# Weight tiles that start at 64 or 192 bytes from the moving operand, output projections by 256 columns, and the dilated q, k, v units by two matmuls of 256

## The chip, the cores and the metric

The kernel runs on one core of one Trainium2 chip. The metric is the device time of one execution in microseconds (us); the time of the kernel before is the median of three.

## What is computed

The input is 256 tokens of width 1024 in float32. Two blocks of two layers each follow one another. Shortened from the reference:

```python
def first_block(x, ...):                       # two layers
    h = rms_norm(x, norm_mix[l]);  proj = h @ w_in[l]
    y_a = dilated_attention(dq, dk, dv) @ w_proj_a[l]      # 3 dilations x 4 heads of 64
    y_b = stick_breaking_attention(sq, sk, sv) @ w_proj_b[l]
    x = x + (gates_a * y_a + gates_b * y_b) @ w_out[l]
    x = x + conv_ffn(rms_norm(x, norm_ffn[l]), w_up, conv_w, conv_b, w_down)   # 1024 -> 2*2816 -> 1024
def second_block(x, mem, ...):                 # layer 0 even_mixer, layer 1 odd_mixer
    x = x + rms_norm_2(mixer(rms_norm_2(x, g[0])), g[1])
    x = x + rms_norm_2(memory_cross_attention(h, mem, ...), g[3])
    x = x + rms_norm_2(square(relu(h @ mlp_w1[l])) @ mlp_w2[l], g[5])          # 1024 -> 4096 -> 1024
```

## The kernel before

**Layout.** An activation lies transposed: 128 features on the partitions, 256 tokens along the free axis, eight chunks of features for width 1024. A projection multiplies weight chunks (128 x 128, the stationary operand, loaded into TensorE by a LDWEIGHTS) with such chunks (128 x 256, the moving operand that streams past).

**Three matmuls for one product.** Each float32 operand is held as a high part in the type fp32r and a low part, the rest. `mm3` (L240) makes a product of three matmuls: high weight by high activation, low weight by high activation, high weight by low activation. So a chunk of 256 tokens is three matmuls of 256 columns, each with a weight load of its own. Nearly all of TensorE's work comes from `mm` (L236), which `mm3` calls.

**The weight stream.** `plan` writes out every block of weights in the order of use, mostly 512 KB each. `prep` (L188) loads block i into a tile raw by DMA and splits it in two halves: ScalarE copies a half to its high part (L199), VectorE subtracts to get the low part (L200). A half is one tile w of the pool tag "w", which has eight buffers (`WB = 8`). `take` hands a block out and prepares up to five blocks ahead.

**Where the tiles stand.** A buffer of tag "w" is as large as the largest tile that asks for it: 4160 bytes on each partition. The program places the eight at bytes 39552, 43712, 47872, 52032, 56192, 60352, 64512 and 68672, which is 128, 192, 0 and 64 modulo 256, twice over. The activations' high and low parts are tiles xh: four buffers of tag "xs" (the input of w_in, w_up, the mixers and w1), all at 128 modulo 256, and sixteen of tag "hs" (the input of all output projections), all at 64. High and low parts, chunks and column blocks within these tiles lie multiples of 256 bytes apart (but for two units of 260 columns). Below, the *distance* of a pair is the start of the moving operand less that of the stationary operand, modulo 256. Before the change it takes the values 0, 64, 128 and 192 about equally often.

**The output projections** (w_out, w_down, w2, and the last four chunks of the mixers' outputs) run in `proj_tail` (L367): for each of eight output chunks c, k steps over the input chunks. For c below 7, `mm3_wide` (L245) takes two matmuls a step: the high weight by the high and low activation side by side (512 columns), then the low weight by the high activation (256 columns). The result stands in two halves of a PSUM bank, which the part's reader adds: in the first block two VectorE additions (L875, L877), in the second a ScalarE copy and a VectorE addition (L1343, L1344). Chunk 7 goes by `mm3`.

**The dilated q, k, v units** (`proj_n` with C = 512, called by `unit`, L697) have it the other way round: the activation's chunk of 128 tokens is stationary and 512 columns of the weight stream past, three matmuls of 512 columns a step.

**Order.** The tile framework schedules all engines' instructions by a simulated timeline, so the order in the source is not the order in the queues. Where attention runs, transposes, scores and sums in plain float32 stand between the matmuls of the projections; in w_up, w_down, w1 and w2 the projections' matmuls follow each other by hundreds.

Of the kernel before, what the change touches and what calls it, by code (L numbers as in the profile page):

```python
# [33 lines left out]
LEAD = 5  # L34
WB = 8
TCARGS = dict(schedule_with_timeline_sim=True)
SET_EXP = "natural_log_exp_and_others"
# [78 lines left out]
def starts(blocks):  # L116

    out = [0]
    for _, _, nk, _, C in blocks:
# [3 lines left out]

BUFS = {"x": 5, "xs": 4, "hs": 16, "ft": 7, "sq": 2, "p": 6, "bias": 3, "row": 4, "sm": 16, "mk": 2, "mv": 2,
        "mm": 2, "sc": 2, "pT": 2, "pv": 1, "ms": 1}
# [3 lines left out]
def net(ctx, tc, A, out):  # L129
# [5 lines left out]
    pp = ctx.enter_context(tc.tile_pool(name="psum", bufs=1, space=PSUM))  # L135
    dp = ctx.enter_context(tc.tile_pool(name="dram", bufs=1, space=DRAM))

    def f(x):
# [49 lines left out]
    def prep(i, pieces=1):  # L188
# [7 lines left out]
        for a, b in ((0, h), (h, nk)):  # L196
            if a < b:
                w = wp.tile([P, 2, b - a, C], F32R, tag="w", name=f"w{i}", bufs=WB)
                act.activation(w[:, 0], raw[:, a:b], AF.Copy)  # L199
                dve.tensor_tensor(w[:, 1], raw[:, a:b], f(w[:, 0]), op=OP.subtract)  # L200
                ready[i] += [w[:, :, k] for k in range(b - a)]
# [38 lines left out]
    def mm3(o, l, r, start, stop=True):  # L240

        for n, (a, b) in enumerate(((0, 0), (1, 0), (0, 1))):
            mm(o, l[:, a], r[:, b], start and n == 0, stop and n == 2)

    def mm3_wide(o, l, r, start, stop):  # L245

        mm(o, l[:, 0], r, start, False)
        mm(o[:, 0:T], l[:, 1], r[:, 0], False, stop)

# [73 lines left out]

    def proj_wide(name, c0, x, k, tag):

        ps = bank(tag, "mw")
        for k0 in range(0, k, 8):
            w = take(name, c0, k0)
            for kk in range(min(8, k - k0)):
                mm3_wide(ps.rearrange("p a t -> p (a t)"), w[kk], x(k0 + kk), start=(k0 + kk == 0),  # L330
                         stop=(k0 + kk == k - 1))
        return ps

    def proj_n(name, c0, x, C=256, tag="mm"):

        if C <= 256:
            ps = bank(tag, "mm")
            outs = [ps[:, 0], ps[:, 1]]
        else:
            outs = [bank(tag, "mm", (C,)), bank(tag, "mm", (C,))]  # L340
        step = 2 if C > 260 else 4
        for k0 in range(0, KC, step):
            w = take(name, c0, k0)
            for kk, i in order(step):
                k = k0 + kk
                mm3(outs[i], cut(x(k), col(i)), w[kk], start=(k == 0 and (i == 0 or C > 256)), stop=(k == KC - 1))
        return outs
# [18 lines left out]

    def proj_tail(name, x, k, on_part, tags=("mm", "sc", "mm", "sc", "mm", "sc", "mm", "sc"), first=0):  # L367

        for c in range(first, 8):
            if c == 4:  # L370
                hold(True)
            if c < 7:
                ps = proj_wide(name, 128 * c, x, k, tags[c])
                on_part(c, ps[:, 0], ps[:, 1])
            else:
                on_part(c, proj_c(name, 128 * c, x, k, tags[c]), None)

# [235 lines left out]


    h = Split("xs")
    for c in range(8):
        split_last = h.chunk(c, x[c // 2][:, c % 2], vcol(V_MIX + c))

    def first_sums():
# [5 lines left out]
        return ns  # L625

    exchange = const("exchange", [P, P], nc.gpsimd)
    table = const("table", [32, 28], nc.gpsimd)
# [39 lines left out]
    for l in range(DEPTH):  # L668
        vb = l * V_L1
        w_in = f"w_in{l}"  # L670
        def rope_unit(nat):
            ra = sb("sm", "ra", (2, 4, 2, 8))
            rb = sb("sm", "rb", (2, 4, 2, 8))
            for i in range(2):
# [190 lines left out]
        def residual(w, y, k, gains):  # L865
# [4 lines left out]

            def on_part(c, a, b):
                if c % 2 == 0:
                    xn.append(sb("x", f"x{c // 2}"))
                t = xn[c // 2][:, c % 2]
                state["block1"] = dve.tensor_tensor(t, x[c // 2][:, c % 2], a, op=OP.add).ins  # L875
                if b is not None:
                    dve.tensor_tensor(t, t, b, op=OP.add)  # L877
                if c < 6 and c % 2:
                    ns.pair(xn[c // 2])
                if hn is not None:  # L880
                    hn.chunk(c, t, gains(c))
                if c >= 6:
                    ns.chunk(t)

# [75 lines left out]

    lprod = sb("sm", "lp", (64,))
    lsum = sb("sm", "ls", (2,))
# [347 lines left out]
    class Output:  # L1310
# [24 lines left out]

        def part(self, c, a, b):
            if b is None:
                self.chunk(c, a)
                return
            if c % 2 == 0:  # L1340
                self.ys.append(sb("ft", "y"))
            y = self.ys[c // 2]
            act.activation(y[:, c % 2], b, AF.Copy)  # L1343
            dve.tensor_tensor(y[:, c % 2], a, y[:, c % 2], op=OP.add)  # L1344
            if c == 6:
                self.sums.chunk(y[:, 0])
                self.scale(y[:, 0], y[:, 0], c)
            elif c % 2:
                self.sums.pair(y)
                for i in range(2):  # L1350
                    self.scale(y[:, i], y[:, i], c - 1 + i)

# [16 lines left out]
    for l in range(DEPTH):  # L1369
        name, oo, of = even(h, nrm) if l == 0 else odd(h, nrm)  # L1370
        y = Output(lambda c: gain2(l, 1, c), 2)
        for j in range(2):
            y.pair(j, of.banks[j])
        proj_tail(name, oo, KC, y.part, tags=(None,) * 4 + ("sc", "mm", "sc", "mm"), first=4)
        r = y.sums.rows(1)
# [158 lines left out]
```

## Time and profile before

| | us |
|---|---|
| median of 3 runs | 1434.24 (1433.52 to 1435.65) |
| the profiled execution, its own time | 1434.43 |
| its span, first to last instruction | 1432.3 |
| TensorE busy in the span | 1388.8 (97%) |
| VectorE busy | 1019.8 (71%) |
| ScalarE busy | 886.3 (62%) |

The span lies 2.1 us inside the execution's own time, and that time is 0.2 us from the median. A matmul's row in the profile gives how long one takes from its start to its end; matmuls overlap, so what one adds to the time is the spacing of the starts, which a stretch's length over its count gives.

### The profile page before, as it was taken

How to read it: one execution, taken by the hardware profiler on the slowest of the kernel's cores; microseconds unless marked ns; L12 is line 12 of the kernel's file. 1: busy time of each engine (PE TensorE's matmuls, PEld its weight loads, DVE VectorE, ACT ScalarE, POOL GpSimd, SP SyncE). 2: the span in 40 equal slices, each digit the busy share in tenths (PEclk: the TensorE clock that was granted, in tenths of full speed). 3: DMA queues.
4: the chain of work that ended last, by engine and by line, in shares of the span. 5: the costliest groups of instructions: out<-in, count | busy, mean ns of one | idle time of the engine just before them, and what ended most of it. 6: DMA issues, size and time to landing. Idle time of an engine off the chain costs nothing.

```text
span 1432.3 us, 26226 instructions
## 1 busy us (share of the span) xinstructions
PE 1388.8 (97%) x9950; PEld 1270.7 (89%) x9950; DVE 1019.8 (71%) x2140; ACT 886.3 (62%) x1740; POOL 27.3 (2%) x54
## 2 busy tenths in 40 slices
PE   8999999999999999999999989899999999899997
PEld 6789999998888999999899968799989878799886
DVE  6665888886656578888777786777656876777554
ACT  6666566665566666666656656566556676576553
POOL 1000000000000000000000010000000010000000
PEclk9999999999999999999999989999999999999999
DMA  7543566556653455656655553266656534265662
GB/s 247 187 124 119 182 195 191 188 177 188 192 170 119 127 172 188 193 190 198 198 167 164 154 139 118 75 190 186 186 187 180 161 94 133 82 186 189 182 189 85
DMA packets 69326, 236.14 MB, mean 165 GB/s; under 512 B 7954, under 2 KB 12322, under 8 KB 69200
## 3 DMA queue, kind: packets, MB, share of 16 engines
q1 hardware_dynamic: 67136, 229.24, 51.6%
q0 software_dynamic: 1920, 5.04, 1.8%
q8 instruction: 78, 1.28, 0.4%
q14 instruction: 48, 0.39, 0.1%
q10 hardware_dynamic: 144, 0.19, 0.0%
HBM read 233.35 MB, written 1.09 MB: 164 GB/s over the span
## 4 chain that ended last, share of the span: by engine, by line
issue 53%; PE 39%; DVE 3%; ACT 3%; DMA 1%; POOL 0%; SPq 0%; DVEq 0%; POOLq 0%; ACTq 0%
PE mm L236 21%; PE mw L236 12%; PE mo L236 2%; PE ssum L427 1%; PE pT L483 1%; PE sc L607 1%; PE sc L604 1%; ACT w L199 1%; DVE w L200 1%; PE pv L541 1%; DMA bias<-brel_d 1%; DMA x<-in_xT_dram 0%; ACT rstd L176 0%; ACT sq L431 0%; ACT px L176 0%
## 5 line engine op out<-in xcount | busy, mean ns | idle before, releaser
L200 DVE TENSOR_TENSOR w<-raw,w 128x512 fp32r<-128x512 f32 (+2 forms) x866 | 585.3, 686 | 303.3 <-ACT w L199 292.8
L199 ACT ACTIVATE w<-raw 128x512 fp32r<-128x512 f32 (+2 forms) x866 | 535.5, 626 | 414.6 <-PE mm L236 225.5
L236 PE MATMUL mm<-xh,w 128*128 128x256 f32 x5892 | 722.8, 283 | 7.8 <-ACT xh L1000 6.8
L236 PEld LDWEIGHTS mm<-xh,w 128*128 128x128 f32 x5892 | 703.7, 190 | 21.2 <-ACT xh L1000 8.4
L236 PE MATMUL mw<-xh,w 128*128 128x512 f32 (+1 forms) x1832 | 327.3, 339 | 2.4 <-DVE xh L271 1.4
L236 PEld LDWEIGHTS mw<-xh,w 128*128 128x128 f32 x1832 | 281.2, 188 | 44.6 <-DVE xh L271 2.0
L236 PE MATMUL mm<-w,xh 128*128 128x512 f32 (+2 forms) x672 | 145.8, 372 | 9.5 <-ACT w L199 7.0
L236 PEld LDWEIGHTS mm<-w,xh 128*128 128x128 f32 x672 | 113.6, 191 | 34.0 <-ACT w L199 8.4
L236 PE MATMUL mo<-xh,w 128*128 128x256 f32 x192 | 30.6, 307 | 0.5 <-ACT xh L513 0.5
L236 PEld LDWEIGHTS mo<-xh,w 128*128 128x128 f32 x192 | 26.5, 206 | 4.4 <-ACT xh L513 1.7
L1000 ACT ACTIVATE xh<-x,vec 128x256 fp32r<-128x256 f32 x48 | 22.6, 501 | 10.4 <-DVE x L1365 9.9
L497 POOL DMA_DIRECT2D bias<-brel_d x28 | 14.9, 538 | 680.0 <-DVE sbb L821 293.0
L905 ACT ACTIVATE ftt<-fa,vec 128x256 f32<-128x256 f32 x44 | 24.1, 594 | 2.3 <-DVE fa L900 0.5
L1003 DVE SCALAR_TENSOR_TENSOR xh<-x,vec,xh 128x256 fp32r<-128x256 f32 x48 | 22.1, 483 | 1.1 <-ACT xh L1000 1.1
L431 ACT ACTIVATE sq<-x 128x512 f32<-128x512 f32 x33 | 20.4, 617 | 2.3 <-DMA x<-in_xT_dram 2.1
L906 DVE SCALAR_TENSOR_TENSOR ftt<-fa,vec,ftt 128x255 f32<-128x255 f32 x44 | 20.9, 482 | 0.2
L907 DVE SCALAR_TENSOR_TENSOR ftt<-fa,vec,ftt 128x254 f32<-128x254 f32 x44 | 21.0, 477 | 0.0
L703 DVE TENSOR_TENSOR gate<-mm,rstd 128x512 f32<-128x512 f32 x16 | 11.1, 691 | 12.5 <-PE mm L236 12.5
L438 DVE TENSOR_TENSOR sq<-sq 128x512 f32<-128x512 f32 x26 | 17.9, 688 | 0.0
L176 ACT ACTIVATE ftt<-ftt 128x512 f32<-128x512 f32 x22 | 13.9, 631 | 6.4 <-DVE ftt L907 6.4
L1364 DVE TENSOR_TENSOR y<-y,rstd 128x512 f32<-128x512 f32 (+1 forms) x25 | 14.5, 581 | 4.3 <-ACT rstd L176 4.1
L910 DVE TENSOR_TENSOR fa<-mm,rstd 128x512 f32<-128x512 f32 x22 | 15.1, 687 | 3.1 <-PE mm L236 3.1
(413 smaller groups left out, 1137.2 us busy)
## 6 DMA issues: line engine op xcount, KB each, us to landing
raw<-in_wt_dram SPq DMA_DIRECT2D x411, 512.0 KB, 3.6
raw<-in_wt_dram SPq DMA_DIRECT2D x16, 384.0 KB, 3.5
bias<-brel_d POOLq DMA_DIRECT2D x28, 128.0 KB, 3.4
raw<-in_wt_dram SPq DMA_DIRECT2D x4, 520.0 KB, 3.5
mem<-in_memT_dram SPq DMA_DIRECT2D x8, 256.0 KB, 4.2
x<-in_xT_dram SPq DMA_DIRECT2D x4, 256.0 KB, 6.7
raw<-in_wt_dram SPq DMA_DIRECT2D x4, 256.0 KB, 3.3
out_dram<-y SPq DMA_DIRECT2D x4, 256.0 KB, 2.5
```

The costliest lines, as they stand in the source:

```text
L199: act.activation(w[:, 0], raw[:, a:b], AF.Copy)
L200: dve.tensor_tensor(w[:, 1], raw[:, a:b], f(w[:, 0]), op=OP.subtract)
L236: i = pe.matmul(o, a, b, start=start, stop=stop, skip_group_check=True).ins
L431: act.activation(sq, src, AF.Square)
L438: dve.tensor_tensor(self.acc, self.acc, sq, op=OP.add)
L497: nc.gpsimd.dma_start(o, src)
L905: act.activation(t[:, c], a[:, c], AF.Identity, bias=vcol(vb + V_CB + ch), scale=w[2])
L906: dve.scalar_tensor_tensor(t[:, c, 1:], a[:, c, :T - 1], w[1], t[:, c, 1:], op0=OP.mult, op1=OP.add)
L907: dve.scalar_tensor_tensor(t[:, c, 2:], a[:, c, :T - 2], w[0], t[:, c, 2:], op0=OP.mult, op1=OP.add)
L910: dve.tensor_tensor(a, o, over(rr), op=OP.mult)
L1000: act.activation(hi, t, AF.Copy, scale=g)
L1003: return dve.scalar_tensor_tensor(lo, t, g, f(hi), op0=OP.mult, op1=OP.subtract)
```

## The change

Four edits. The buffers of tag "w" become 1056 floats, 4224 bytes, and every weight tile is a view of one (`W_SLOT`). Two padding tiles, 192 and 64 bytes, go ahead of the activations' pools, and small scratch tiles get a tag of their own ("ro"). `proj_tail` uses `mm3` for all chunks and lets two chunks share a bank, so that chunks 0 to 5 are read out in pairs and 6 and 7 each alone. `proj_n` splits 512 columns into two times 256.

```diff
-BUFS = {..., "sm": 16, "mk": 2, ...
+W_SLOT = 1056
+BUFS = {..., "sm": 16, "ro": 4, "mk": 2, ...
...
+    def pad(name, n):
+        ap.tile([P, n // 4], F32, tag=name, name=name, bufs=1)
...
-                w = wp.tile([P, 2, b - a, C], F32R, tag="w", name=f"w{i}", bufs=WB)
+                w = wp.tile([P, W_SLOT], F32R, tag="w", name=f"w{i}", bufs=WB)
+                w = w[:, :2 * (b - a) * C].rearrange("p (s k c) -> p s k c", s=2, k=b - a)
...
                 k = k0 + kk
-                mm3(outs[i], cut(x(k), col(i)), w[kk], start=(k == 0 and (i == 0 or C > 256)), stop=(k == KC - 1))
+                for a in range(0, C, 256 if C > 260 else C):
+                    s = slice(a, a + (256 if C > 260 else C))
+                    mm3(outs[i][:, s], cut(x(k), col(i)), cut(w[kk], s),
+                        start=(k == 0 and a == 0 and (i == 0 or C > 256)), stop=(k == KC - 1))
...
-    def proj_tail(name, x, k, on_part, tags=("mm", "sc", "mm", "sc", "mm", "sc", "mm", "sc"), first=0):
+    def proj_tail(name, x, k, on_part, tags=("mm", "sc", "mm", "sc", "mm"), first=0):
+        tags = list(tags)
+        cs, ps = [], None
         for c in range(first, 8):
             if c == 4:
                 hold(True)
-            if c < 7:
-                ps = proj_wide(name, 128 * c, x, k, tags[c])
-                on_part(c, ps[:, 0], ps[:, 1])
-            else:
-                on_part(c, proj_c(name, 128 * c, x, k, tags[c]), None)
+            if not cs:
+                ps = bank(tags.pop(0), "mw", (2, T) if c < 6 else (1, T))
+            for k0 in range(0, k, 8):
+                w = take(name, 128 * c, k0)
+                for kk in range(min(8, k - k0)):
+                    mm3(ps[:, len(cs)], w[kk], x(k0 + kk), start=(k0 + kk == 0 and not cs),
+                        stop=(k0 + kk == k - 1))
+            cs.append(c)
+            if c % 2 or c >= 6:
+                on_part(cs, ps)
+                cs = []
...
+    pad("pad0", 192)
     h = Split("xs")
...
+    pad("pad1", 64)
...
-                state["block1"] = dve.tensor_tensor(t, x[c // 2][:, c % 2], a, op=OP.add).ins
-                if b is not None:
-                    dve.tensor_tensor(t, t, b, op=OP.add)
+                s = slice(c % 2, c % 2 + len(cs))
+                state["block1"] = dve.tensor_tensor(xn[c // 2][:, s], x[c // 2][:, s], ps, op=OP.add).ins
...
-            act.activation(y[:, c % 2], b, AF.Copy)
-            dve.tensor_tensor(y[:, c % 2], a, y[:, c % 2], op=OP.add)
```

After the change the program places the eight weight buffers at 39552, 43776, 48000 and so on to 69120, which is 128 and 0 modulo 256 in turn, and all twenty xh buffers at 64. So the distance is 64 or 192, whichever of the two operands streams (again but for the 260-column units).

TensorE's queue in the second weight block of an output chunk of w_down, layer 0, before the change (output bank, then stationary and moving tile; the first number after w is the block):

```order
L236 MATMUL mw_4066<-xh_2892,w109_3966 128x512
L236 MATMUL mw_4066<-xh_2892,w109_3966 128x256
L236 MATMUL mw_4066<-xh_2892,w109_3966 128x512
L236 MATMUL mw_4066<-xh_2892,w109_3966 128x256
L236 MATMUL mw_4066<-xh_3037,w109_3966 128x512
L236 MATMUL mw_4066<-xh_3037,w109_3966 128x256
```

The same place after the change, where w109_4307 and w109_4310 stand at 128 and w110_4333 at 0 modulo 256:

```order
L242 MATMUL mw_4431<-xh_3177,w109_4307 128x256 x6
L242 MATMUL mw_4431<-xh_3322,w109_4307 128x256 x6
L242 MATMUL mw_4431<-xh_3467,w109_4310 128x256 x6
L242 MATMUL mw_4431<-xh_3612,w109_4310 128x256 x6
L242 MATMUL mw_4431<-xh_3757,w110_4333 128x256 x6
```

A step over one input chunk was a matmul of 512 and one of 256 columns with two weight loads; it is three of 256 with three.

Six halves of weight blocks in w_up, layer 0, before the change, in TensorE's queue. The program places w65_2463 at 64 modulo 256, w65_2466 and w66_2495 at 192, w66_2498 at 128, w67_2538 at 0 and w67_2541 at 64, the moving xh at 128:

```order
L236 MATMUL mm_2605<-xh_2037,w65_2463 128x256 x12
L236 MATMUL mm_2605<-xh_2086,w65_2466 128x256 x12
L236 MATMUL mm_2680<-xh_1920,w66_2495 128x256 x12
L236 MATMUL mm_2680<-xh_1982,w66_2498 128x256 x12
L236 MATMUL mm_2680<-xh_2037,w67_2538 128x256 x12
L236 MATMUL mm_2680<-xh_2086,w67_2541 128x256 x12
```

The same after the change; w65_2748, w65_2751, w67_2823 and w67_2826 stand at 128, w66_2780 and w66_2783 at 0 modulo 256, the moving xh at 64:

```order
L242 MATMUL mm_2890<-xh_2339,w65_2748 128x256 x12
L242 MATMUL mm_2890<-xh_2371,w65_2751 128x256 x12
L242 MATMUL mm_2965<-xh_2203,w66_2780 128x256 x12
L242 MATMUL mm_2965<-xh_2278,w66_2783 128x256 x12
L242 MATMUL mm_2965<-xh_2339,w67_2823 128x256 x12
L242 MATMUL mm_2965<-xh_2371,w67_2826 128x256 x12
```

The instructions and their order are the same there; what moved is the distance, from 64, 192, 192, 0, 128, 64 to 192, 192, 64, 64, 192, 192.

## Rows read from the trace of the kernel before

**Rows 1.** The page's first part: busy us, share of span, instructions.

```profile
PE 1388.8 (97%) x9950; PEld 1270.7 (89%) x9950; DVE 1019.8 (71%) x2140; ACT 886.3 (62%) x1740; POOL 27.3 (2%) x54
```

**Rows 2.** Whom TensorE waited for: total us, times, longest us.

```profile
PE mm L236 <- ACT w L199: 7.5, 4, 6.1
PE mm L236 <- ACT xh L1000: 6.8, 5, 2.5
```

**Rows 3.** Windows: length; busy (count) of PE, PEld, DVE, ACT, POOL; clock; DMA share, GB/s.

```profile
200.52:313.11 112.59, 112.59 (x961) 112.59 (x961) 96.86 (x165) 72.77 (x123) 1.62 (x3) 1.00 0.59 187
313.20:367.22 54.02, 54.02 (x310) 47.22 (x309) 36.79 (x67) 29.94 (x54) 0.00 (x0) 1.00 0.61 185
562.10:676.20 114.10, 113.97 (x978) 113.77 (x977) 97.19 (x166) 75.28 (x127) 0.00 (x0) 1.00 0.60 188
938.90:1015.50 76.60, 76.60 (x653) 76.55 (x652) 56.95 (x86) 52.15 (x87) 0.00 (x0) 1.00 0.62 188
1015.53:1094.41 78.88, 78.88 (x450) 68.75 (x449) 43.66 (x68) 42.15 (x73) 0.00 (x0) 1.00 0.62 187
1253.90:1331.00 77.10, 77.10 (x652) 77.07 (x651) 56.77 (x86) 52.07 (x87) 0.00 (x0) 1.00 0.60 186
```

**Rows 4.** Windows, PE alone: w66_2495, w66_2498, w67_2538, w67_2541, twelve matmuls each.

```profile
228.76:230.12 1.36, 1.36 (x15) 1.00 0.73 268
230.12:231.56 1.44, 1.44 (x15) 1.00 0.48 97
231.56:232.98 1.42, 1.42 (x15) 1.00 0.79 271
232.98:234.39 1.41, 1.41 (x14) 1.00 0.53 99
```

**Rows 5.** Windows in w1 of layer 0, twelve matmuls each: distances 192, 64, 192, 64.

```profile
949.34:950.76 1.42, 1.42 (x15) 1.00 0.72 188
950.76:952.17 1.41, 1.41 (x15) 1.00 0.60 244
952.17:953.53 1.36, 1.36 (x14) 1.00 0.35 121
953.53:954.89 1.36, 1.36 (x14) 1.00 0.87 268
```

**Rows 6.** Windows, twelve matmuls each at distance 192: a gate unit, w1 of layer 1.

```profile
498.06:499.47 1.41, 1.41 (x14) 1.00 0.20 29
1255.83:1257.24 1.41, 1.41 (x15) 1.00 0.75 288
```

**Rows 7.** Window: 24 matmuls of 512 columns in dilated units, layer 1.

```profile
375.11:380.67 5.56, 5.56 (x27) 1.00 0.67 198
```

**Rows 8.** TensorE's groups by form: busy us, mean ns of one, idle before.

```profile
L236 PE MATMUL mm<-xh,w 128*128 128x256 f32 x5892 | 722.8, 283 | 7.8 <-ACT xh L1000 6.8 <-ACT w L199 0.5 <-DVE xh L1003 0.4
L236 PE MATMUL mw<-xh,w 128*128 128x512 f32 x916 | 323.6, 397 | 2.4 <-DVE xh L271 1.4 <-ACT y L1321 0.5 <-DVE mx L1196 0.5
L236 PE MATMUL mm<-w,xh 128*128 128x512 f32 x480 | 120.4, 405 | 7.0 <-ACT w L199 7.0
L236 PE MATMUL mo<-xh,w 128*128 128x256 f32 x192 | 30.6, 307 | 0.5 <-ACT xh L513 0.5
L236 PE MATMUL mm<-ox,w 128*128 128x256 f32 x96 | 13.6, 298 | 1.0 <-ACT ox L509 1.0
```

**Rows 9.** Windows: the even mixer with its cross attention, then the odd.

```profile
746.20:938.90 192.70, 178.12 (x1286) 159.42 (x1286) 144.02 (x398) 118.49 (x286) 8.86 (x17) 0.96 0.45 131
1094.30:1253.90 159.60, 149.79 (x1096) 131.44 (x1094) 120.07 (x321) 105.58 (x264) 8.82 (x16) 0.99 0.43 124
```

**Rows 10.** VectorE's and ScalarE's groups by form that read the wide banks.

```profile
L877 DVE TENSOR_TENSOR x<-x,mw 128x256 f32<-128x256 f32 x28 | 11.7, 417 | 0.1
L875 DVE TENSOR_TENSOR x<-x,mw 128x256 f32<-128x256 f32 x28 | 11.7, 417 | 4.5 <-PE mw L236 4.5
L1343 ACT ACTIVATE y<-mw 128x256 f32<-128x256 f32 x20 | 7.7, 384 | 0.0
```

More of the change, by code (lines that the diff above doesn't have):

```diff
@@ L121, in starts @@
     return out
-BUFS = {"x": 5, "xs": 4, "hs": 16, "ft": 7, "sq": 2, "p": 6, "bias": 3, "row": 4, "sm": 16, "mk": 2, "mv": 2,
+BUFS = {"x": 5, "xs": 4, "hs": 16, "ft": 7, "sq": 2, "p": 6, "bias": 3, "row": 4, "sm": 16, "ro": 4, "mk": 2, "mv": 2,
         "mm": 2, "sc": 2, "pT": 2, "pv": 1, "ms": 1}
@@ L243, in mm3 @@
             mm(o, l[:, a], r[:, b], start and n == 0, stop and n == 2)
-    def mm3_wide(o, l, r, start, stop):
-        mm(o, l[:, 0], r, start, False)
-        mm(o[:, 0:T], l[:, 1], r[:, 0], False, stop)
     def cut(w, s):
@@ L322, in proj_c @@
         return ps
[L324 to L332, printed above, removed]
     def proj_n(name, c0, x, C=256, tag="mm"):
@@ L671, in rope_unit @@
         def rope_unit(nat):
-            ra = sb("sm", "ra", (2, 4, 2, 8))
-            rb = sb("sm", "rb", (2, 4, 2, 8))
+            ra = sb("ro", "ra", (2, 4, 2, 8))
+            rb = sb("ro", "rb", (2, 4, 2, 8))
             for i in range(2):
@@ L869, in residual, with on_part @@
             xn = []
-            def on_part(c, a, b):
+            def on_part(cs, ps):
+                c = cs[0]
                 if c % 2 == 0:
                     xn.append(sb("x", f"x{c // 2}"))
-                t = xn[c // 2][:, c % 2]
-                state["block1"] = dve.tensor_tensor(t, x[c // 2][:, c % 2], a, op=OP.add).ins
-                if b is not None:
-                    dve.tensor_tensor(t, t, b, op=OP.add)
-                if c < 6 and c % 2:
-                    ns.pair(xn[c // 2])
[L880 to L883, printed above, removed]
+                s = slice(c % 2, c % 2 + len(cs))
+                state["block1"] = dve.tensor_tensor(xn[c // 2][:, s], x[c // 2][:, s], ps, op=OP.add).ins
+                if c < 6:
+                    ns.pair(xn[c // 2])
+                for c in cs:
+                    t = xn[c // 2][:, c % 2]
+                    if hn is not None:
+                        hn.chunk(c, t, gains(c))
+                    if c >= 6:
+                        ns.chunk(t)
             proj_tail(w, y, k, on_part)
@@ L958, in net @@
     hm = mem_operand(0, mem)
-    lprod = sb("sm", "lp", (64,))
+    lprod = sb("ro", "lp", (64,))
     lsum = sb("sm", "ls", (2,))
@@ L1334, in chunk, with part @@
             self.scale(self.ys[3][:, c % 2], ps, c)
[L1336 to L1342, printed above, removed]
-            act.activation(y[:, c % 2], b, AF.Copy)
-            dve.tensor_tensor(y[:, c % 2], a, y[:, c % 2], op=OP.add)
[L1345 to L1351, printed above, removed]
+        def part(self, cs, ps):
+            if len(cs) == 2:
+                self.pair(cs[0] // 2, ps)
+            else:
+                self.chunk(cs[0], ps[:, 0])
     def close(y, r):
@@ L1373, in net @@
             y.pair(j, of.banks[j])
-        proj_tail(name, oo, KC, y.part, tags=(None,) * 4 + ("sc", "mm", "sc", "mm"), first=4)
+        proj_tail(name, oo, KC, y.part, tags=("sc", "mm", "sc"), first=4)
         r = y.sums.rows(1)
```

## The prediction, written before the changed kernel ran

> **What bounds the kernel now.** I read the shares first: TensorE is busy for 97% of the span, VectorE for 71%, ScalarE for 62% [rows 1]. Then the waits: the two largest of TensorE's add up to 14.3 us, and the first falls where the weight stream starts [rows 2]. Then the windows over the long stages, in their order in time w_up, w_down, w_up of the next layer, w1, w2, w1 of the next [rows 3]. In five of the six TensorE is busy from edge to edge, at the full clock (granted 1.00), while VectorE has 14% or more left. So what one matmul adds there, the spacing of the starts, is the time. A window's count includes the two matmuls under way at its left edge. w_up has 959 starts in 112.59 us, 117.4 ns each; the four windows of w_up and w1 together 380.39 us for 959 + 976 + 651 + 650 = 3236, which is 117.55 ns. In w_down seven chunks take 7 x 22 = 154 steps in 54.02 us, 350.8 ns a step of 512 and 256 columns; in w2 224 steps in 78.88 us, 352.1 ns; together 351.6.
>
> Last I cut w_up at the edges of the weight halves, with the names and places that the program gives them. Twelve equal matmuls take 1.36, 1.44, 1.42 and 1.41 us at distances 192, 0, 128 and 64: 113.3, 120.0, 118.3 and 117.5 ns [rows 4]. Nothing differs but the place of the weight tile, and the four lengths come back in every later unit of that stage. So the distance between the two operands costs time here.
>
> Distance alone doesn't fix the spacing. At 192 and 64 there are two rhythms, a fast one of 113.3 ns and a slow one of 117.5 ns. In w1 of layer 0 (w288_10834, w289_10906, w289_10909, w290_10938) distance 192 begins slow after 128, 64 goes on slow, the next 192 turns fast, and the next 64 stays fast, though 64 in w_up was slow [rows 5]. Where 64 and 192 meet, the trace behaves like that at nearly all places: out of the fast rhythm no such step falls back, and a slow 64 ahead of a 192 turns fast, with few exceptions. One is a gate unit that began slow after a break and stayed slow through 64 and 192 [rows 6]. In w1 of layer 1, 192 comes after 0 and is slow [rows 6].
>
> **The change part by part.** The new places leave only 64 and 192. Distances 0 and 128, at 118 to 120 ns, go; and a stretch should reach the fast rhythm within one or two weight halves and keep it until something else than a projection breaks it.
>
> *Matmuls of 256 columns in the long stretches.* w_up has 22 units of 48 in two layers, 2112; w1 2 x 16 x 48 = 1536; the gates 2 x 8 x 48 = 768; the last chunk of w_out, w_down and w2, 3 x (8 + 22 + 32) x 2 = 372. Sum 4788, each from 117.55 to 113.3 ns: 4.25 x 4788 = 20.3 us less.
>
> *The output projections.* Their 2 x 7 x (8 + 22 + 32) = 868 steps go from 351.6 ns to 3 x 113.3 = 340, so 11.6 x 868 = 10.1 us less. The third weight load is in that price already, since each of the twelve matmuls behind 113.3 ns has one of its own. The Trainium skill, TensorE: Matmul & The Clock Gate, section Back-to-back issue gap, gives columns by 2.4 GHz plus 2.5 ns for a matmul, so 215.8 and 109.2 ns. By that, three of 256 would be 2.5 ns dearer than the pair and this edit would cost some 2 us; the trace disagrees, with 117.55 for 109.2 and 351.6 for 325.
>
> *The other 256s.* 5892 + 192 + three groups of 96 (one is shown) less 4788 are 1584 matmuls [rows 8], and 48 steps in the mixers' tails. They are broken up by attention's own matmuls, so I take half the gain, 2.1 ns, 3.3 us, with 0.3 us for the tails. In the mixers TensorE also waits for others (14.6 us in the even one, 9.8 us in the odd [rows 9]), and a faster matmul there partly waits longer: I keep 2.5 us. Bounds 0 and 7.2 us.
>
> *The dilated units.* 480 matmuls of 512 columns [rows 8] at 5.56 us for 24, 231.7 ns [rows 7]. Two of 256 are 226.6 in the fast rhythm and 235 in the slow one: between 2.4 us less and 1.6 us more. With transposes between them I take the middle, 0. That a weight tile streams by here and not the activation, the trace shows for no long row of 256 columns; the bounds hold for that too.
>
> *Reading out.* 28 pairs of additions of 417 ns become single ones over 512 columns, and 20 copies of 384 ns go [rows 10]. TensorE is busy from edge to edge in w_down and w2 [rows 3], so this work is covered; the last two chunks are read singly as before, so the end of each stage keeps its chain. If that cover were gone, six stage ends at one 0.42 us addition would give 2.5 us; I take 0. The pair waits for its second chunk, a step count that the next two chunks' matmuls cover, and it holds one bank where two chunks held two.
>
> *What spoils it.* Each break starts a stretch anew, mostly slow for 12 to 24 matmuls: 0.05 to 0.1 us each, for some 20 breaks that touch the long stretches 2 us.
>
> Sum: 20.3 + 10.1 + 2.5 + 0 + 0 - 2 = 30.9 us, off the profiled execution's 1434.4 (0.2 us from the median): 1403.5, rounded up to **1404**.
>
> **The rivals.** *The slow rhythm holds (slower).* If a stretch that starts slow stays slow under 64 and 192 alone, as the gate unit did [rows 6], everything runs at 117.6 ns: no gain on the 4788, steps at 352.8 for 351.6 (1.0 us), dilated units 1.6 us, the others about 0.5 us, the third weight load and the split being the price that is left: 1434.4 + 3.5 = 1438. It decides if the first blocks of w_up and w1 are slow and two changes of distance don't lift them. For it: three or four such places in the trace. Against it: the same two changes lifted w1 in each unit [rows 5].
>
> *Half of it.* Each of the four long runs (w_up with w_down, w1 with w2, in two layers) is entered once and can lock either way. Two of four slow give back half of 20.3 + 10.1 less the gates' 3.3, about 13 us: 1417.
>
> *The place is no cause.* The Trainium skill, SBUF — State Buffer, section Who interferes with whom, says that TensorE never waits on another engine for its reads, and TensorE's page gives the streaming and the loading operand a read port each. Rows 4 speak against reading that as "the place doesn't matter". If the four lengths had another cause in step with the weight buffers, every 256 stays at 117.55: steps 352.65 for 351.6, 0.9 us, dilated units 480 x 3.4 ns = 1.6 us: 1437.
>
> *Another engine becomes the bound.* VectorE is busy 96.86 of 112.59 us in w_up [rows 3]; at 113.3 ns the stretch would be 108.7 us and VectorE at 89%. If w_up couldn't shorten, 2 x 4.5 us come back: 1413. Against it: no row of the waits names VectorE's weight half, and an 11% margin with blocks prepared up to five ahead is enough.
>
> **How the numbers follow.** Chances: forecast 0.68, for which 1395 to 1412 is the range (upper bounds of the other 256s and of the dilated units, no breaks: 1434.4 - 30.4 - 7.2 - 2.4 = 1394.4; the other end, breaks twice as dear and mixers without gain plus 1.6 us: 1410). Half 0.14, VectorE 0.05, slow rhythm 0.08, no cause 0.05. The range from 1395 to 1428 leaves out the last two and the edges. Within 0.2% (2.9 us, about what a measurement of this kernel tells from no change) I put half of "no cause" and some of "slow rhythm" and "half": 0.05; slower 0.09, faster 0.86.
>
> **What would show it.** In the windows: w_up's 959 starts in about 109 us, w2's 224 steps in about 76.5 us, w1 in about 74 us for the same 651 starts; twelve matmuls of one weight half at 1.36 us nearly everywhere, none at 1.44. The dilated window of 5.56 us between 5.44 and 5.64. VectorE's busy time down by some 5 us. Wrong would be: whole stages at 1.41 (the slow rhythm), 1.44 still there (place is no cause), or idle gaps of TensorE ahead of weight tiles in w_up (VectorE).

## The result and the profile after

The changed kernel takes 1414.84 us, the median of four runs (1411.67 to 1415.26), against 1433.88 us (1433.16 to 1435.65) before: a ratio of 0.9861 with a 95% interval of 0.9843 to 0.9878, or 19.0 us less. Forecast were 30.4 us less. The profiled execution is the shortest of the four: 1411.67 us, with a span of 1409.9 us; its mean granted clock is 0.992, that of the other three, at 1414.45 to 1415.26 us, 0.988 to 0.990. So the trace shows about 3 us more gain than the median.

The page's shares after (busy us, share of span, instructions), against [rows 1]:

```profile
PE 1360.1 (96%) x11346; PEld 1304.4 (93%) x11346; DVE 1002.6 (71%) x2080; ACT 881.0 (62%) x1720; POOL 27.7 (2%) x54
```

VectorE has 17.2 us less work, more than the 5 us of the forecast: its 28 pairs of additions (23.4 us, [rows 10]) became 12 additions over 512 columns and 8 over 256 (11.5 us), and 20 more in the second block (8.4 us), which the forecast did not count, are gone. But it was not the bound. The long stages in windows, against [rows 3] (length; busy and count of PE, PEld, DVE, ACT, POOL; clock; DMA share, GB/s), in the order w_up, w_down, w_up of layer 1, w1, w2, w1 of layer 1:

```profile
209.52:312.86 103.34, 103.34 (x912) 103.34 (x912) 89.37 (x153) 68.53 (x114) 1.63 (x3) 1.00 0.65 195
312.86:365.22 52.36, 52.36 (x464) 52.36 (x463) 34.18 (x58) 30.15 (x54) 0.00 (x0) 1.00 0.60 192
560.77:671.50 110.73, 110.73 (x980) 110.73 (x979) 96.86 (x166) 74.37 (x126) 0.00 (x0) 1.00 0.64 195
933.75:1005.39 71.64, 71.64 (x632) 71.64 (x631) 54.53 (x83) 50.48 (x84) 0.00 (x0) 1.00 0.61 193
1005.39:1081.56 76.17, 76.17 (x675) 76.17 (x674) 41.63 (x62) 39.89 (x67) 0.00 (x0) 1.00 0.63 194
1238.00:1311.80 73.80, 73.80 (x653) 73.80 (x652) 56.46 (x86) 51.65 (x87) 0.00 (x0) 1.00 0.64 198
```

The first holds 910 starts, so 113.6 ns each (117.4 before). w_down makes its 154 steps in 52.36 us and w2 its 224 in 76.17, both 340.0 ns a step (351 and 352 before). In w_up of layer 1 it is 113.3 ns; in w1 113.7 and 113.5. TensorE is busy from edge to edge in all six, and VectorE is at 86 and 87% in w_up, where 89% was forecast.

The weight halves of w66 and w67, twelve matmuls each (PE alone), against [rows 4]:

```profile
231.26:232.62 1.36, 1.36 (x14) 1.00 0.75 265
232.62:233.98 1.36, 1.36 (x14) 1.00 0.53 105
233.98:235.34 1.36, 1.36 (x14) 1.00 0.72 277
235.34:236.70 1.36, 1.36 (x14) 1.00 0.25 96
```

What was 1.36, 1.44, 1.42 and 1.41 is 1.36 four times. So the gain that was looked for is there in the long stages, and something else takes part of it back. To find it, the spacings of TensorE's starts are summed over the whole program in both traces, each spacing counted to the stage of the matmul that it begins with:

| change of the spacings, us | |
|---|---|
| w_up, w_down, w1, w2 of both layers | -25.5 |
| matmuls of 256 in w_in (gates among them, -4.2), w_pa, w_pb | -4.3 |
| mixers and cross attention, their projections | -3.9 |
| the dilated units' own matmuls (layer 0: 61.4 to 64.2; layer 1: 57.0 to 57.8) | +3.6 |
| w_out, two layers (23.5 to 24.5 and 24.6) | +2.1 |
| dilated scores sd (13.2 to 17.2) | +4.0 |
| other plain float32 matmuls | +1.3 |

They add up to -22.7 us; the spans, which reach a little beyond the first and the last matmul, differ by 22.4. Four rows go the wrong way, the dilated units, w_out and sd by 9.7 us together.

*w_out.* Windows over it before (layer 0), and after in both layers:

```profile
163.81:187.36 23.55, 22.83 (x139) 20.05 (x137) 21.76 (x45) 15.02 (x29) 0.00 (x0) 1.00 0.61 189
```

```profile
166.41:190.92 24.51, 22.68 (x195) 22.14 (x193) 21.13 (x38) 16.07 (x31) 0.00 (x0) 1.00 0.61 190
526.24:550.88 24.64, 22.81 (x195) 22.28 (x194) 21.14 (x38) 16.07 (x31) 0.00 (x0) 1.00 0.60 187
```

TensorE's idle time in the window goes from 0.72 to 1.83 us. The list of waits says for whom (total us, times, longest us), against 1.4 us on this tile before [rows 8]:

```profile
PE mw L242 <- DVE xh L272: 3.7, 4, 1.3
```

The matmuls wait for the mixed activations that VectorE still makes. Before, the chunks 0 to 3 had a bank each, and TensorE could work on four chunks with the inputs that were there. After, chunk 1 stands behind the whole of chunk 0 in their common bank, and chunk 3 behind chunk 2: in layer 0 the first matmul of chunk 1 starts 10.0 us into the stage, where before it was the first of all. So TensorE runs out of work.

*The dilated scores.* TensorE's timeline (start us, us, operation, count) before and after at the same place:

```profile
70.60 1.14 PE L758 MATMUL sd<-qTs 64*128 64x256 f32 x8
```

```profile
69.53 1.13 PE L763 MATMUL sd<-qTs 64*128 64x256 f32 x4
```

Each of these matmuls leaves two records. Eight records took 1.14 us, now four take 1.13. A score matmul uses 64 partitions, head 0 the lower half and head 1 the upper half, and where both heads' stood next to each other their records start in pairs, 6 to 15 ns apart in the trace. In TensorE's queue, before and after (output bank, then moving and stationary tile, in this order here and in the queues shown ahead; sd_707 and sd_901 are one head, sd_708 and sd_902 the other):

```
L758 MATMUL sd_707<-qTs_326,qTs_447 128x256
L758 MATMUL sd_707<-qTs_326,qTs_568 128x256
L758 MATMUL sd_708<-qTs_326,qTs_447 128x256
L758 MATMUL sd_708<-qTs_326,qTs_568 128x256
```

```
L763 MATMUL sd_901<-qTs_376,qTs_545 128x256
L763 MATMUL sd_901<-qTs_376,qTs_714 128x256
L242 MATMUL mm_930<-w17_741,xh_120 128x256
L242 MATMUL mm_929<-w18_770,xh_125 128x256 x4
L763 MATMUL sd_902<-qTs_376,qTs_545 128x256
L763 MATMUL sd_902<-qTs_376,qTs_714 128x256
```

Now five projection matmuls stand between the heads, and each head's scores run alone. TensorE is busy either way, so no wait shows it; the group's busy time does, 8.8 us before and 12.4 after for the same 48 records (24 matmuls) of 411 ns:

```profile
L758 PE MATMUL sd<-qTs 64*128 64x256 f32 x48 | 8.8, 411 | 0.0
```

```profile
L763 PE MATMUL sd<-qTs 64*128 64x256 f32 x48 | 12.4, 411 | 0.0
```

The Trainium skill, TensorE: Matmul & The Clock Gate, section The mechanism (of packing small matmuls), says that matmuls at different tile positions of the array overlap; the trace agrees (starts 6 to 15 ns apart) while they are neighbours in the queue.

### The profile page after: what moved, and what is told of

It reads as the page before. It is cut to its first block, busy times and chain, and to the rows that moved or that the text cites. A ratio compares the mean times of both kernels' runs of the same rounds, so it can differ in the third digit from the quotient of the medians.

```text
span 1409.9 us, 28955 instructions
## 1 busy us (share of the span) xinstructions
PE 1360.1 (96%) x11346; PEld 1304.4 (93%) x11346; DVE 1002.6 (71%) x2080; ACT 881.0 (62%) x1720; POOL 27.7 (2%) x54
## 4 chain that ended last, share of the span: by engine, by line
issue 54%; PE 36%; DVE 5%; ACT 4%; DMA 1%; POOL 0%; SPq 0%; DVEq 0%; POOLq 0%; ACTq 0%
PE mm L242 18%; PE mw L242 13%; PE mo L242 1%; PE ssum L430 1%; ACT w L205 1%; DVE w L206 1%; DMA bias<-brel_d 1%; PE pT L486 1%; PE pv L544 1%; ACT y L1327 0%; DMA x<-in_xT_dram 0%; ACT rstd L181 0%; ACT sq L434 0%; PE sc L610 0%; ACT px L181 0%
## 5 line engine op out<-in xcount | busy, mean ns | idle before, releaser
L242 PE MATMUL mm<-xh,w 128*128 128x256 f32 x5472 | 651.1, 279 | 7.9 <-ACT xh L1006 6.9
L242 PEld LDWEIGHTS mm<-xh,w 128*128 128x128 f32 x5472 | 634.4, 188 | 19.3 <-ACT xh L1006 8.7
L242 PE MATMUL mw<-xh,w 128*128 128x256 f32 x3168 | 367.7, 277 | 3.7 <-DVE xh L272 3.7
L242 PEld LDWEIGHTS mw<-xh,w 128*128 128x128 f32 x3168 | 363.4, 188 | 6.0 <-DVE xh L272 4.5
L242 PE MATMUL mm<-w,xh 128*128 128x256 f32 (+1 forms) x1152 | 149.1, 287 | 10.7 <-ACT w L205 7.6
L242 PEld LDWEIGHTS mm<-w,xh 128*128 128x128 f32 x1152 | 141.2, 193 | 16.3 <-ACT w L205 7.8
L763 PE MATMUL sd<-qTs 64*128 64x128 f32 (+1 forms) x96 | 18.6, 350 | 0.0
L906 DVE TENSOR_TENSOR fa<-mm,rstd 128x512 f32<-128x512 f32 x22 | 15.2, 691 | 4.0 <-ACT w L205 3.9
L916 DVE TENSOR_TENSOR fa<-mm,rstd 128x512 f32<-128x512 f32 x22 | 15.1, 684 | 2.8 <-PE mm L242 2.7
```

Of the source, the lines that this page charges most:

```text
L242: i = pe.matmul(o, a, b, start=start, stop=stop, skip_group_check=True).ins
L763: j = pe.matmul(s[m][:, g - gs[0]], half(qT[g], hp, m)[:, col(i)], half(kT[g], hp, m)[:, :n], start=(g == gs[0]), stop=True, skip_group_ch ...
L906: dve.tensor_tensor(a, o, over(rr), op=OP.mult)
```

## The experiments

Theory: the places gain by leaving distances 0 and 128 and by a change of rhythm, and by nothing else; the split of the projections is worth its 340 ns steps where nothing breaks it; what is missing is lost by shared banks in w_out and by the order around the dilated units. Rivals are named in each expectation. The kernel before was run beside each group and took 1435.06 us in the first, 1435.49 in the second, 1435.72 in the third. The changed kernel was not run beside them: its 1414.84 us stand beside 1433.88 before, so differences to it are uncertain by 1 to 2 us on top of their spread. All edits are shortened.

**The new places alone** (`place`): the old `proj_tail` and 512 columns. Against the kernel before:

```diff
+W_SLOT = 1056
...
+                w = wp.tile([P, W_SLOT], F32R, tag="w", name=f"w{i}", bufs=WB)
...
+    pad("pad0", 192)
...
+    pad("pad1", 64)
```

> The new places of the weight and xh tiles alone, with the old pair of 512 and 256 columns in the output projections and the old 512 in the dilated units. Theory (the distance costs time, and the split only lets the output projections reach the fast rhythm): w_up and w1 as in the changed kernel (w_up 109 us for 959 starts, 113.5 ns each), the pair of the output projections still 350 to 352 ns, so 868 steps without their 10 us: 1424 to 1427. Rival (the split is the cause, the places are not): 1434, w_up at 117.4 ns.

1417.8 us (1416.88 to 1420.68), ratio 0.9885 (0.987 to 0.9899): 17.3 us less, more than the theory said. Windows over w_up (960 starts), w_down, and the first seven chunks of w2 (224 steps):

```profile
200.60:309.80 109.20, 109.20 (x962) 109.18 (x961) 95.73 (x165) 73.13 (x124) 1.63 (x3) 1.00 0.59 192
309.80:371.90 62.10, 62.10 (x376) 55.12 (x375) 42.41 (x77) 34.64 (x62) 0.00 (x0) 1.00 0.61 187
1004.20:1083.30 79.10, 79.10 (x451) 68.84 (x450) 43.77 (x68) 42.16 (x73) 0.00 (x0) 1.00 0.62 186
```

w_up reaches 113.7 ns. w_down and w2 keep their pair of 512 and 256 columns, at 353 ns, so the new places are worth nothing to it. Of the change's 19.0 us the places alone give nearly all, and everything else together only some 3 us (1417.8 against 1414.84), though by it w_down goes from 62.1 and 61.8 to 59.8 us twice and w2 from 90.2 to 87.0 twice, 10.7 us less.

**The split alone** (`split`): the places of before. Against the changed kernel, as in all edits from here on where nothing else is said:

```diff
-                w = wp.tile([P, W_SLOT], F32R, tag="w", name=f"w{i}", bufs=WB)
...
+                w = wp.tile([P, 2, b - a, C], F32R, tag="w", name=f"w{i}", bufs=WB)
...
-    pad("pad0", 192)
...
-    pad("pad1", 64)
```

> The split alone: output projections and dilated units by 256 columns, tiles at the old places (distances 0, 64, 128, 192). Theory: every 256 stays at 117.5 ns, steps at 352.6 for 351.6, so 1434 to 1437, no faster than before. Rival (the split is the cause): w_down and w2 steps at 340 to 345 ns and 1415 to 1425.

1445.5 us (1441.88 to 1448.28), ratio 1.0072 (1.0049 to 1.0095): slower than before, and slower than the theory's 1434 to 1437. w_down (layer 0) and w_up (layer 1) stay at their old lengths:

```profile
318.80:380.70 61.90, 61.90 (x531) 61.90 (x530) 39.43 (x67) 34.80 (x62) 0.00 (x0) 1.00 0.60 188
561.40:685.80 124.40, 124.40 (x1062) 124.29 (x1062) 103.98 (x178) 80.81 (x137) 0.00 (x0) 1.00 0.63 186
```

A third matmul of 256 pays only at 113.3 ns, and most of what lies above the old time is lost in the stages named above, which the theory had not counted: sd takes 17.2 us, 4.0 more than before, w_out 1.3 and 1.4 us more, w_in of layer 0 2.7 us more.

This kernel also tells the distance from the place itself, since its moving tiles stand at 64 in some stages and at 128 in others. Within its stretches of one distance the mean spacing is 119.8 ns at distance 0 in both cases and 118.5 ns at 128 in both, and at 64 and 192 it lies between the two rhythms, at 115.4 to 115.7 ns.

**Distances 0 and 128** (`d0_128`):

```diff
-    pad("pad0", 192)
+    pad("pad0", 256)
```

> The changed kernel with 64 bytes more of padding, so that the weight tiles stand at distances 0 and 128 from the xh tiles instead of 64 and 192. Theory: 120.0 and 118.3 ns, a mean of 119.2, in every long stage; against 117.5 before that is 1.7 ns on 6384 matmuls, 6 ns on 916 steps and 6 ns on 480 dilated pairs, some 19 us, of which waits take a part: 1444 to 1455. Rival (regular buffers or the split do it, whatever the distance): 1412 to 1418.

1459.75 us (1457.58 to 1460.84), ratio 1.0172 (1.0156 to 1.0187), 5 us more than the theory's upper end. w_up of layer 1 and w2:

```profile
569.60:696.10 126.50, 126.50 (x1062) 126.39 (x1061) 104.48 (x177) 80.84 (x137) 0.00 (x0) 1.00 0.62 183
1038.80:1130.40 91.60, 91.60 (x771) 91.60 (x770) 50.54 (x79) 48.28 (x85) 3.28 (x4) 1.00 0.58 184
```

w2's 768 matmuls take 91.6 us, 119.2 ns each, against 113.3: one number in the source, the same instructions in the same order, 45 us. That ends the rival that the place is no cause. The Trainium skill, SBUF — State Buffer, section Who interferes with whom, gives TensorE's two read ports as independent of each other; these windows show that their places matter all the same (119.2 against 113.3 ns), since nothing else differs.

**192 alone** (`d192`): every weight buffer at 128 modulo 256.

```diff
-W_SLOT = 1056
+W_SLOT = 1088
```

> The changed kernel with weight buffers of 4352 bytes, all at distance 192 where the activation streams (64 where the weight streams). Theory A (a distance of 64 or 192 is enough, since the fast rhythm is reached from any start): long stages at 113.3 ns, 1411 to 1418. Theory B (a slow 192 needs the change of distance to turn fast): each long stretch keeps the rhythm in which it began, whole stages at 1.41 us for twelve matmuls, 1418 to 1436.

1423.7 us (1420.33 to 1425.74), ratio 0.992 (0.9901 to 0.9939). Windows over w_up, w_down, w_up of layer 1, w2:

```profile
209.80:317.10 107.30, 107.30 (x913) 107.30 (x913) 90.41 (x153) 68.35 (x114) 1.63 (x3) 1.00 0.64 189
317.10:379.30 62.20, 62.20 (x531) 62.20 (x530) 39.51 (x67) 34.74 (x62) 0.00 (x0) 1.00 0.60 187
565.40:679.10 113.70, 113.70 (x1005) 113.70 (x1004) 98.06 (x168) 77.09 (x130) 0.00 (x0) 1.00 0.64 192
1012.50:1099.60 87.10, 87.10 (x771) 87.10 (x770) 50.20 (x79) 48.20 (x85) 3.28 (x4) 1.00 0.62 192
```

In layer 0 w_up runs at 117.8 ns (911 starts) and w_down with it, 1439 matmuls in one rhythm; in layer 1 1530 matmuls run at 113.3. The time lies in theory B's range, and in all four long runs one distance keeps a stretch in the rhythm in which it began; three of the four began fast.

**64 alone** (`d64`): as `d192`, with activations at 192 modulo 256.

```diff
-    pad("pad0", 192)
+    pad("pad0", 320)
```

> The changed kernel with all weight buffers at 128 and all activations at 192 modulo 256: distance 64 where the activation streams. Theory A: a stretch that begins at 64 begins slow, and only a step to 192 lifts it; so the long stages stay at 117.5 ns, w_up at 124, w_down at 62, w2 at 90 us, and the total is 1414.8 + about 25, 1436 to 1442. Rival: 64 alone is as good as 192 alone (d192: three of five long stretches fast): 1418 to 1428.

1431.47 us (1426.78 to 1439.69, twelve runs), ratio 0.9976 (0.9958 to 0.9993): between the two expectations. Five of the runs have the same mean granted clock, 0.989, and lie from 1426.78 to 1439.69 us, so the clock does not make this spread; whether other stretches lock from one execution to the next is not shown, since one was profiled. w_up of both layers, w1 and w2:

```profile
210.20:317.50 107.30, 107.30 (x912) 107.30 (x912) 90.26 (x153) 68.26 (x114) 1.63 (x3) 1.00 0.63 187
566.40:685.00 118.60, 118.60 (x1010) 118.60 (x1009) 99.31 (x168) 77.69 (x130) 0.00 (x0) 1.00 0.61 184
950.40:1021.80 71.40, 71.40 (x632) 71.40 (x631) 54.61 (x83) 50.29 (x84) 0.00 (x0) 1.00 0.63 194
1021.80:1108.90 87.10, 87.10 (x771) 87.10 (x771) 50.08 (x79) 48.30 (x85) 3.28 (x4) 1.00 0.62 192
```

w_up is slow throughout in both layers, as the theory said; but w1 and w2 are at 113.3 ns, with no step to 192 in them. The theory's "a stretch that begins at 64 begins slow" falls: which rhythm a stretch takes is settled at the break before it, at 64 as at 192; what in the break settles it was not tried. Both in turn did what neither does alone: in the changed kernel the last break in each of the four long runs is followed by the fast rhythm within 55 matmuls, to the end of the run. In the seven other kernels that have both in turn the matmuls of 256 columns in the long runs do the same, within 77 matmuls each time.

**The heads' scores in turn** (`sdpair`):

```diff
                             behind(j, "sc")
+                            if last_sd is not None:
+                                no_sync(j, last_sd)
```

> The changed kernel, with one addition: the dilated attention's score matmuls (sd, 128 columns or 256, two heads on the two halves of the partitions) are held in the order head 0, head 1, head 0, head 1. Theory A: these matmuls run at the same time when the two heads' follow each other in the queue (starts some 6 to 15 ns apart in the trace of before) and one after the other (some 200 to 320 ns) when both of one head come first; so their summed spacing falls from 17.2 us to 13 to 14.5 us and the time by about 3 us, to 1410 to 1412. Rival: the 4 us more of these matmuls is waiting that would turn up elsewhere; then sd falls, the total stays at 1414 to 1415.

1412.05 us (1411.05 to 1413.14), ratio 0.9838 (0.9814 to 0.9861), 2.8 us under the change. But the summed spacing of sd is 16.0 us, not 13 to 14.5: the chain orders the heads and lets projections stand between them. The 128-column scores gain (6.3 to 4.7 us busy), those of 256 columns don't (12.4, now 12.9). The total agrees with theory A, but its range overlaps that of the change (from 1411.67), and sd accounts for 1.2 of the 2.8 us; so this run decides little. The alternation that the theory asks for is not what counts either: in the queue before the change, shown above, both matmuls of one head come first, and the records run in pairs all the same. What the pairs have in common is that nothing stands between the heads; `dil512`, below, bears on that.

**A bank for each chunk of w_out** (`wout`):

```diff
-                ps = bank(tags.pop(0), "mw", (2, T) if c < 6 else (1, T))
+                ps = bank(tags.pop(0), "mw", (2, T) if c < alone else (1, T))
...
-            if c % 2 or c >= 6:
+            if c % 2 or c >= alone:
...
-            proj_tail(w, y, k, on_part)
+            proj_tail(w, y, k, on_part, **(dict(tags=("mm", "sc") * 4, alone=0) if k == KC else {}))
```

> The changed kernel, but w_out's eight chunks have a bank each, read singly; w_down and w2 as in the change. Theory A: with two chunks in one bank TensorE runs out of work ahead of the last mixed activations (waits for DVE xh of 1.6 and 0.9 us in each layer, 1.0 us once before the change); with banks of their own chunks 0 to 3 fill the time again, w_out falls from 24.5 to 22.5 to 23 us in each layer and the time by 2 to 4 us, to 1411 to 1413. Rival: the mixing on VectorE itself has become later, and the wait is as long whoever has the banks: w_out stays at 24 to 24.5 us, the total at 1414 to 1415.

1409.09 us (1408.58 to 1411.6), ratio 0.982 (0.9796 to 0.9845), 5.7 us under the change and 2 us under theory A's range. w_out in both layers, and its wait:

```profile
166.80:189.30 22.50, 22.00 (x195) 21.81 (x194) 20.84 (x41) 15.33 (x30) 0.00 (x0) 1.00 0.64 198
524.90:547.40 22.50, 22.00 (x194) 21.81 (x193) 20.82 (x40) 15.13 (x30) 0.00 (x0) 1.00 0.66 195
```

```profile
PE mw L242 <- DVE xh L272: 1.0, 2, 0.5
```

24.5 and 24.6 become 22.5 each, 4.1 us, and the wait goes from 3.7 to 1.0 us. VectorE's work is not later: in both kernels TensorE resumes with the second tile of mixed activations 3.5 us after the stage began, but here it has work for longer until then. Theory A holds; 1.6 us of the 5.7 have no place in this reading.

**The dilated units by 512 again** (`dil512`):

```diff
-                for a in range(0, C, 256 if C > 260 else C):
...
+                mm3(outs[i], cut(x(k), col(i)), w[kk], ...
```

> The changed kernel with the dilated q, k, v units as before, by matmuls of 512 columns. Theory A: two of 256 there take turns of fast and slow and cost 231 ns a pair, as much as one of 512, so the units are worth 0 to 1 us; the order of the score matmuls is lost through the schedule as a whole, not through this split: sd stays at 16 to 17 us, the total at 1413 to 1416. Rival: the split is what pulls the score matmuls apart and thins the queue at the start: sd comes back to 13 to 14 us and the start's half-clock spell goes, the total is 1409 to 1411.

1405.73 us (1403.56 to 1409.41), ratio 0.9795 (0.9768 to 0.9822), 9.1 us under the change. My theory A fell here and its rival held, though the time is 3 us below the rival's range too: the split does pull the scores apart. The place of the timeline above, in this kernel:

```profile
71.12 1.14 PE L760 MATMUL sd<-qTs 64*128 64x256 f32 x8
```

Eight in 1.14 us again; sd is back to 13.2 us, and w_in of layer 0 goes from 121.6 to 119.3 us. What the start has to do with that is open. Windows over the first 40 us, of the change and of this kernel:

```profile
0.00:40.00 40.00, 31.97 (x233) 31.31 (x234) 26.11 (x86) 26.75 (x56) 6.98 (x16) 0.96 0.77 248
```

```profile
0.00:40.00 40.00, 31.88 (x134) 25.29 (x135) 25.37 (x80) 26.78 (x56) 6.98 (x16) 1.00 0.77 245
```

TensorE is idle equally long in both, 8.0 and 8.1 us. What differs is the granted clock, which falls to its lower level (1.2 GHz) for a while in the change, after TensorE has waited. But not every kernel with the split shows this: in `wout` and `sdpair` the clock there is 1.00, and `wout` spends as long in the dilated units of layer 0 (64.5 us) as the change (64.2); with 512 columns they take 61.4.

Some of the 9.1 us may be the clock: three of this kernel's five runs have a mean of 0.993, which no run of the change has. Runs of the two kernels within 0.001 of each other in mean clock differ by 6 to 9 us.

**The dilated split on top of the places alone** (`place_dil`):

```diff
 # the kernel `place`, and in proj_n
+                for a in range(0, C, 256 if C > 260 else C):
...
```

> The kernel with the new places alone, plus the dilated units by two matmuls of 256 columns; all output projections as before the change. Theory A: the split there pulls the two heads' score matmuls apart in the queue and costs 4 to 9 us by itself, sd at 16 to 17 us: 1422 to 1427 (the new places alone took 1417.8). Rival: it costs that only together with the new output projections, whose schedule it meets; alone it is worth what its matmuls say, and the time is 1416 to 1419 with sd at 13.2 us.

1424.11 us (1421.37 to 1426.7), ratio 0.9923 (0.9905 to 0.9941), 6.3 us over `place`. sd is 17.2 us again (13.2 in `place`), so the split of the dilated units by itself breaks the pairs, whatever the output projections do:

```profile
L769 PE MATMUL sd<-qTs 64*128 64x256 f32 x48 | 12.4, 411 | 0.0
```

**The split in w_down and w2 alone** (`hyb`): the new `proj_tail` for k = 22 and 32, all else as `place`.

```diff
 # the kernel `place`, with the change's proj_tail beside the old one, as proj_pairs
+            (proj_tail if k == KC else proj_pairs)(w, y, k, on_part if k == KC else on_pair)
...
```

> The new places of the change, and the three matmuls of 256 columns with shared banks in w_down and w2 alone; w_out, the mixers' tails and the dilated units as before the change. Theory A: the split of the projections is worth 2.0 to 2.3 us in each w_down and 3.2 us in each w2, and what was given back came from w_out, the mixers and the order of the score matmuls: 1417.8 of the kernel with the new places alone less 10.7 is 1407 (1404 to 1410). Rival: the rest of the program loses by any change of w_down and w2 (their ends, read out in pairs, or the schedule made anew), and it stays at 1412 to 1416 like the changed kernel.

1408.84 us (1404.35 to 1411.23), ratio 0.9811 (0.9784 to 0.9839): 9.0 us under `place`, of 10.7 expected. w_down of layer 0:

```profile
308.87:368.70 59.83, 59.83 (x530) 59.83 (x529) 39.38 (x67) 34.65 (x62) 0.00 (x0) 1.00 0.63 195
```

The two big projections keep what their steps promise.

**Both losses undone** (`wout_dil`): `wout` and `dil512` together.

> The changed kernel with two parts of it undone: the dilated units by matmuls of 512 columns, and w_out's chunks with a bank each. Theory A: the two losses are apart in time and add up: from dil512's 1405.7, the 2 x 2 us of w_out come off, 1401 to 1403, with sd at 13.2 us and w_out at 22.5 us in each layer; the prediction's two large terms are then there in full. Rival: the gain of either is partly waiting that the other takes up (the start's weight stream, VectorE's work ahead of w_up), and the time stays at 1404 to 1407.

1405.62 us (1404.41 to 1406.44), ratio 0.9795 (0.9777 to 0.9812): no better than `dil512`, as the rival's number has it. The stages did what theory A said (w_out 22.5 us in both layers, sd 13.2), and by the end of w_down in layer 1 this kernel is 4.5 us ahead (721.7 against 726.2). It is lost again in the mixers. Windows over the even and the odd one, first `dil512`, then this kernel:

```profile
726.20:908.90 182.70, 165.06 (x1242) 147.01 (x1241) 136.58 (x392) 113.46 (x274) 8.77 (x17) 0.98 0.46 136
1085.60:1216.30 130.70, 121.22 (x903) 103.85 (x901) 96.80 (x274) 85.52 (x222) 6.00 (x12) 1.00 0.41 124
```

```profile
721.70:907.20 185.50, 167.02 (x1243) 148.63 (x1241) 136.83 (x392) 113.59 (x274) 9.40 (x17) 0.96 0.46 134
1084.00:1216.80 132.80, 123.84 (x903) 106.17 (x901) 96.97 (x274) 85.50 (x222) 6.01 (x12) 0.97 0.42 123
```

The same matmuls keep TensorE busy 4.6 us longer, with a granted clock of 0.96 and 0.97 for 0.98 and 1.00. The mean clock is 0.988 or 0.989 in all four of its runs and 0.993 in three of the five of `dil512`, whose one run at 0.988 took 1409.4 us. At 0.988 and 0.989 this kernel is 3 to 5 us faster than that one run, which is what theory A asks for. That the mixers' waits fell worse for the clock is argued from this; it was not tried by itself.

## Why the prediction was right, and 10.8 us off

The change is faster, by 19.0 us of the 30.4 forecast. The time, 1414.84 us, lies inside the wider range, to 1428, and 2.8 us above the forecast's own, 1395 to 1412.

- *What bounds the kernel*, and that distance and rhythm set the spacing: right, shown by `place`, `d192`, `d64` and `d0_128`.
- *Matmuls of 256 in the long stretches* and *the output projections*: right where nothing breaks them. By the prediction's own prices w_up, w1, w_down and w2 should give 3972 x 4.25 ns + 756 x 11.6 ns = 25.7 us (3972 being 2112 + 1536 + 324 of the last chunks); they gave 25.5 in the trace.
- *The output projections, in w_out*: wrong. 112 steps should have given 1.3 us and cost 2.1. The step that failed is in *Reading out*: "it holds one bank where two chunks held two" was seen and priced at nothing, with a cover read in w_down and w2, where TensorE is busy from edge to edge. In w_out it waits (3.7 us in the two layers), and there the cover is gone; undoing it gave 4.1 us by the windows.
- *The dilated units*: the term that failed most. 0, bounded by 2.4 us less and 1.6 us more, counted only their own matmuls, which in the window that answers to [rows 7] behave so:

```profile
372.70:378.30 5.60, 5.60 (x50) 1.00 0.67 198
```

  48 in 5.60 us, 233 ns a pair, inside the forecast 5.44 to 5.64. Twelve matmuls at distance 64, twelve at 192, and the next twelve at 64 show why it is no less:

```profile
374.12:375.53 1.41, 1.41 (x14) 1.00 0.72 261
375.88:377.24 1.36, 1.36 (x14) 1.00 0.84 298
377.24:378.65 1.41, 1.41 (x14) 1.00 0.19 76
```

  Here, where the weight streams and the activation is stationary, 64 falls back at once out of the fast rhythm that 192 had reached, with no break between them; the prediction had read, from rows in which the activation streams, that no such step falls back. But the split of these units costs 6.3 us (`place_dil`) to 9.1 us (`dil512`), the latter perhaps with some clock in it: 4.0 us in the scores, whose order it changes, up to 3.6 us in the units (2.8 of it in layer 0, of which the cause stays open), and the rest not located. The bound was one of durations; the order was not read.
- *The other 256s*: 2.5 us forecast. The table's second and third rows are 8.2 us; less the 4.2 us of the gates, forecast apart at 3.3, 4.0 us are theirs, inside the bounds of 0 and 7.2.
- *What spoils it*: 2 us for breaks were too many. In the four long runs 0.2 us of 25.7 are missing; w1 at 113.7 and 113.5 for 113.3 ns is 0.25 us and less each.
- *The rivals*: the slow rhythm held in no long run with both distances in turn; "half of it", at 1417, is 2 us from the measured time, but that is chance: all four long runs lock fast, and what is missing is lost elsewhere. `d192` is that rival's case, with one long run locked slow. VectorE did not become the bound.

With the dilated split undone the time is 1405.7 us, beside 1404 forecast. In the long stages the places and the projections are worth what was worked out for them; that the total agrees so well is in part luck: in the trace of `dil512` w_out and the gates are 3.8 and 1.3 us short of the forecast, while the other 256s give 3.2 us more than forecast and the breaks take about 1 us of their 2.

## What to carry to other kernels

Where TensorE is the bound, cut a long stage at the edges of its weight tiles and compare equal matmuls: if their lengths follow the tiles' addresses, padding can be worth more than restructuring (here 17.3 us by the places alone, 9.0 more by the new w_down and w2 in `hyb`), and two good places in turn are safer than one (1414.84 us with both, 1423.7 and 1431.47 with one). An edit whose own matmuls cost nothing still moves all that the scheduler places around them: read in the queue what stands beside the small matmuls that share the array, and which chunks are open where TensorE waits for an input. Try the edits of a change one by one, since here one part cost 6 to 9 us of the 30 that the others gave.

## What the runs showed of the hardware

- The spacing of 256-column matmuls in fp32r depends on the two operands' distance modulo 256: 119.2 ns with 0 and 128 (`d0_128`), 113.3 or 117.8 with 64 or 192. It is the distance and not either place: with moving tiles at 64 or at 128 the spacing at distance 0 is 119.8 ns (`split`).
- Where the activation streams, 64 and 192 each have two lasting rhythms. At 192 one kept 1439 matmuls slow, and the same distance kept 1530 fast later in the same execution (`d192`). I had not expected 64 alone to lock fast, as in w1 and w2 of `d64`. Where the weight streams, in the dilated units, 64 went back to the slow rhythm after 192 had reached the fast one (means over the changed kernel 117.6 and 114.8 ns), so the two in turn don't hold the fast rhythm there.
- Pairs of 512 and 256 columns gain nothing by distances 64 and 192: 352 ns a step in w2 before, 353 with the new places alone.
- Score matmuls on two halves of the partitions run together only as neighbours: eight records in 1.14 us, or four in 1.13.
